# Loading weights later at two places, and additions into y on VectorE at the borders of the down groups

## The chip, the cores and the metric

One core of a Trainium2 chip runs the whole kernel as one program. The metric is the device time of an execution in microseconds (us); lower is better. Five engines work at the same time, each on its own list of instructions, in order: TensorE (PE) multiplies matrices, VectorE (DVE) and ScalarE (ACT) do arithmetic by element, GpSimd (POOL) does as well, and SyncE (SP) issues most of the transfers between device memory and on-chip memory. What one engine hands to another is awaited by semaphores.

## The reference

One step of a one-layer encoder on 1024 prompt frames and 64 sample frames (1088 columns in all, D = 1024), all in float32. Cut to what matters here:

```python
rq, rk, rv, rg, sq, sk, sv, ga, gb = split(rms_norm(x, g_attn) @ w_in)     # projections
A = retention(rope(rq), rope(rk), rv)                                      # 4 heads
B = sliding_window_attention(sq, sk, sv)                                   # 16 heads
x += (sigmoid(ga) * A_out + sigmoid(gb) * B_out) @ w_mix_out
x += cross_attn(x, memory K/V)
x += (silu(hn @ w_gate) * (hn @ w_up)) @ w_down                            # hn = rms_norm(x, g_ffn), D_FF = 2816
y = rms_norm(x, g_final)
```

The first product of the kernel is the retention V of one head, the second the retention K of the same head. The last large product is `@ w_down`, with the sum over the 2816 rows of `w_down` cut into three groups.

## The kernel before

Float32 values are multiplied in three passes: each operand is split into a high half, rounded to TensorE's float32r type by a cast on ACT, and a low half, the difference, by a subtraction on DVE (`split`, lines 122 to 124). A product then is hi x hi + hi x lo + lo x hi (lines 212, 213 and 215). All columns stand transposed, so weights are the stationary operand and the 1088 columns stream past in two halves (`HALF` = 544), each in two parts of 272.

Large products are done on 2x2 blocks: two output tiles by two halves of the columns (t), each a sum over two halves of the inner dimension (j). `plain` (line 232) does the eight block products as they stand, four inner tiles each, six matmuls per tile, so 24 matmuls per block product in the first two groups. `strassen` (line 254) does seven with sums of blocks as operands, and merges their results on DVE and ACT. The operands have names: B11, B12, B21, B22 are blocks, T1 to T4 are sums. The order of a Strassen product is P1 (B11), P2 (B21), P6 (T2), P5 (T1), P7 (T3), P3 (B22), P4 (T4). The weights come as a pair of raw tiles of 512 KB (tag `raw`, two buffers, loaded by SP). For Strassen, `weight_ops` (line 173) splits blocks of them and lets POOL form sums in place in the raw tiles (lines 190, 191, 193 and 196) between the splits: P1 and P2 need none, P7 needs line 190, P5 line 191, P6 line 193 and P3 line 196. Split weights sit in buffers `wq`.

Order: a scheduler lays each engine's list out ahead of time, by priority (order in the program) and by a simulated timeline in which an instruction that is not ready lets later ones pass. `tc.issue_after(ins)` adds that the instructions in its block that run on the engine of `ins` come behind `ins` in that engine's list. It adds no wait.

The start (`project_phase`, line 570, and `start_phase`, line 430): x comes in sixteen tiles (`xr`, four buffers), is scaled on ACT into `xg` and split into the operands. `first` holds the weights of V, split for `plain`; `values(first, 0, self.plain)` multiplies them and stores the four results through SP to `d_qkv` (lines 638 to 641). The next line loads and prepares the weights of K for the first Strassen product: `first = pair("w_k", 0)`.

The down product (`down`, line 1542): the activations of the feed-forward part were stored to `d_op` as ready blocks and sums for each of the three groups (`GROUPS` = 8, 8 and 6 tiles of 128 rows, gi = 0, 1, 2). For each group, m = 0, 2, 4, 6 walks over pairs of output tiles. m = 0 of groups 0 and 1 is `plain`, since it needs only the B operands, and the T operands are loaded behind it (`load_operand`, order T2, T1, T3, T4; each loads tiles `hl` and splits them); the rest is `strassen`. In m = 6 of groups 0 and 1, `refill` replaces each B operand by that of the next group as soon as its product is done (`turn`); B12 takes the place of T4, after the last product. This is the border of two groups. The results are added into `y`: of each emitted pair, one addition reads PSUM and is on DVE (line 1552); the other reads the merged partial result `sb` in SBUF and is on POOL for groups 0 and 1, on DVE for group 2 (line 1554).

Of the kernel before, what the change touches and what calls it, by code (L numbers as in the profile page):

```python
# [2 lines left out]

# [1 line left out]

# [16 lines left out]
KT = D // P  # L22
# [20 lines left out]
OPS = ("B11", "T1", "T2", "B21", "T3", "B22", "T4", "B12")  # L43
# [66 lines left out]
class Kernel:  # L110
# [459 lines left out]
    def project_phase(self):  # L570
        nc, tc, io = self.nc, self.tc, self.io
        with ExitStack() as ctx:
# [7 lines left out]
            first = self.start_phase(sctx)  # L580
# [3 lines left out]
            half = lambda t: slice(t * HALF, (t + 1) * HALF)  # L584
            flat = lambda o: o.rearrange("p b c -> p (b c)")

            def staged():
                count[0] += 1
                return stage[(count[0] - 1) % len(stage)]

            def taken(ps, sb):
                o = staged()
                if sb is None:
                    nc.scalar.copy(o, ps)
                else:
                    nc.vector.tensor_tensor(out=o, in0=ps, in1=sb, op=ALU.add)  # L596
                return flat(o)
# [39 lines left out]

            def values(w, h, by=self.strassen):
                def emit(i, t, ps, sb):
                    self.store(self.d_qkv[2, 2 * h + i, :, half(t)], taken(ps, sb))  # L640
                by(w, self.ops, emit)

            pair = lambda w, h: self.load_ops([io[w][2 * h + i] for i in range(2)])
            def queries(p):
# [8 lines left out]
                        self.store(d[:, 9:17, :], r(o[:, 32:]))  # L653
                return put

            values(first, 0, self.plain)
            first = pair("w_k", 0)
            sctx.close()
            stage, count = self.stage_tiles(), [0]
            with ExitStack() as rctx:  # L660
# [873 lines left out]
    def fetch(self, name, group):  # L1534
        n0 = sum(GROUPS[:group]) // 2
        for k in range(GROUPS[group] // 2):
            self.pools = self.pools[1:] + self.pools[:1]
            a = self.pools[0].tile([P, HALF], F32, tag="hl", name="hl")
            self.load(a, self.d_op[OPS.index(name), n0 + k])
            yield a  # L1540

    def down(self, starts):
        nc, io = self.nc, self.io
        self.rings[0].next = (self.rings[0].next - 2) % KT
        stage = self.ring_tiles(0, 2, "y", F32)
        y = [self.rstd_f] + [stage[i // 2][:, i % 2, :] for i in range(4)]
        y += [self.yp.tile([P, T], F32, name=f"y{i}") for i in range(3)]
        half = lambda m, t: y[m][:, t * HALF:(t + 1) * HALF]
        def add(m, i, t, ps, sb, by=nc.gpsimd):
            v = half(m + i, t).rearrange("p (b c) -> p b c", b=2)  # L1550
            if ps is not None:
                nc.vector.tensor_tensor(out=v, in0=ps, in1=v, op=ALU.add)
            if sb is not None:
                by.tensor_tensor(out=v, in0=sb, in1=v, op=ALU.add)

        begun = set()

        def complete(m, c0, n):
            acc, o = self.rstd[:, c0:c0 + n], y[m][:, c0:c0 + n]
            if c0 not in begun:  # L1560
                begun.add(c0)
                nc.scalar.activation(acc, o, AF.Square)
            else:
                sq = self.hl.tile([P, HALF], F32, tag="hl", name="sq")[:, :n]
                nc.scalar.activation(sq, o, AF.Square)
                nc.vector.tensor_tensor(out=acc, in0=acc, in1=sq, op=ALU.add)

        def load_half(tile, m, a, b):
            self.load(tile.rearrange("p (k m) -> p k m", m=P), io["w_down"][m, :, a:b, :])

        for gi, g in enumerate(GROUPS):
            last = gi == len(GROUPS) - 1
            f0, n = starts[gi], g * P // 2
            for m in range(0, KT, 2):
                def emit(i, t, ps, sb, m=m):
                    add(m, i, t, ps, sb, nc.vector if last else nc.gpsimd)
                    if last and t == 1:
                        complete(m + i, HALF, HALF)

                raws = [self.wp.tile([P, 1024], F32, tag="raw", bufs=2, name="raw") for i in range(2)]  # L1580
                for i in range(2):
                    load_half(raws[i][:, :2 * n], m + i, f0, f0 + g)
                if m == KT - 4 and not last:
                    for name in ("B11", "B21" if gi == 0 else "T2"):
                        self.ahead[name, gi + 1] = list(self.fetch(name, gi + 1))
                if gi == 0:
                    for i in range(2):
                        self.load(y[m + i], self.d_h[1][m + i])
                if m == 0 and not last:
                    self.plain(self.plain_weights(raws, n), self.ops, emit)  # L1590
                    for name in ("T2", "T1", "T3", "T4"):
                        self.load_operand(name, gi)
                else:
                    w = self.weight_ops(raws, n, ("P2", "P4") if last else ())
                    if m == KT - 2 and not last:
                        self.refill = lambda name, gi=gi: self.turn(name, 1) if gi == 0 else self.turn_last(name)
                    self.strassen(w, self.ops, emit, last)
                    self.refill = None
                    if m == 0:
                        for name in ("B21", "T4"):  # L1600
                            self.load_operand(name, gi)
                if last and m == KT - 4:
                    nc.scalar.activation(self.root[:, 0, :1], self.rstd[:, HALF:HALF + 1], AF.Sqrt)
        rest = []
        for m in range(0, KT, 2):
            raw = self.wp.tile([P, 1024], F32, tag="raw", bufs=2, name="raw")
            for i in range(2):
                load_half(raw[:, i * n:(i + 1) * n], m + i, f0 + g // 2, f0 + g)
            ring, slots = self.slots["B11" if m < 4 else "T1"]
            q = self.rings[ring].tile("wb", slot=slots[m // 2 % 2])  # L1610
            self.last_queued = self.split(raw[:, :2 * n], q[:, 0, :2 * n], q[:, 1, :2 * n])
            rest += [(m + i, q[:, :, i * n:(i + 1) * n], self.ops[("B21", "T4")[i]]) for i in range(2)]
        self.finish(y, rest)
# [182 lines left out]
```

## Time and profile before

| | before |
|---|---|
| median of 3 runs | 2211.39 us (2210.66 to 2214.1) |
| profiled execution | 2210.58 us |
| its span, first to last instruction | 2208.8 us |
| mean granted TensorE clock | 0.992 |
| PE busy | 2155.7 us (98%) |
| DVE busy | 1577.8 us (71%) |
| ACT busy | 875.8 us (40%) |
| POOL busy | 653.2 us (30%) |

In the lines of the timeline: start in us from the span's start, duration in us, engine and line of the kernel, operation, output<-input with shapes, count (neighbours of one kind are merged), and in brackets how long the engine had been idle before and what ended that. `SPq` is the issue of a transfer, not the transfer. In the view of groups, busy time and mean ns come first, then idle time and its releasers. In the view of waits: engine and line, whom it waited for, us in total, times, longest. L124 is the low half of any split, L123 the cast.

### The profile page before, as it was taken

To read this page: it belongs to the slowest core of one execution; us is meant where nothing else is said; L and a number is where in the kernel's file an instruction comes from. 1 tells how busy PE (TensorE), PEld (TensorE's weight loads), DVE (VectorE), ACT (ScalarE), POOL (GpSimd) and SP (SyncE) were. 2 spreads that over 40 slices of the span, in tenths; PEclk is the share of its full clock that TensorE was granted. 3 is DMA by queue.
4 is the path that set the end of the run, shared out by engine and by line. 5 is a ranking of instruction groups with operands and counts; after the bars stand their busy time and mean duration, and the time that the engine had idled before them with its cause. 6 is when DMAs were issued, how large, how long until landed. Compare 5 with 4: busy or idle time off the path is not lost.

```text
span 2208.8 us, 41446 instructions
## 1 busy us (share of the span) xinstructions
PE 2155.7 (98%) x16307; PEld 2089.8 (95%) x16307; DVE 1577.8 (71%) x2654; ACT 875.8 (40%) x1894; POOL 653.2 (30%) x442
## 2 busy tenths in 40 slices
PE   8999999999999998999999999999999999999996
PEld 8999999999999996779999999999999999999996
DVE  7996958776677668775455555768777776778498
ACT  7344424344344346553133333333322222344243
POOL 1322333332343122230000000014555555544440
PEclk9999999999999999999999999999999999999998
DMA  5534253445245476327443111422333332385233
GB/s 197 167 127 137 90 149 122 131 127 156 96 153 172 165 220 213 112 64 224 124 153 107 57 49 58 144 86 90 124 133 101 104 118 95 124 297 167 91 114 110
DMA packets 181444, 290.83 MB, mean 132 GB/s; under 512 B 40290, under 2 KB 109314, under 8 KB 181250
## 3 DMA queue, kind: packets, MB, share of 16 engines
q1 hardware_dynamic: 176706, 278.74, 39.5%
q10 hardware_dynamic: 4032, 7.80, 0.9%
q8 instruction: 129, 2.11, 0.4%
q0 software_dynamic: 512, 1.64, 0.2%
q14 instruction: 65, 0.53, 0.1%
HBM read 196.95 MB, written 91.16 MB: 130 GB/s over the span
## 4 chain that ended last, share of the span: by engine, by line
PE 80%; DVE 11%; DMA 4%; ACT 2%; issue 2%; POOL 1%; SPq 0%; DVEq 0%; ACTq 0%; POOLq 0%
PE pq L215 15%; PE pq L212 15%; PE pq L213 15%; PE pd L156 8%; PE pd L158 8%; PE pd L157 8%; DVE wq L124 1%; PE pout L1031 1%; PE pss L969 1%; DMA hl<-d_op 1%; DVE T L124 1%; DVE B L124 1%; PE pp L1008 1%; DMA qs<-d_qkv 1%; DVE stage L596 1%
## 5 line engine op out<-in xcount | busy, mean ns | idle before, releaser
L124 DVE TENSOR_TENSOR wq<-raw,wq 128x512 fp32r<-128x512 f32 (+1 forms) x499 | 441.2, 888 | 137.1 <-ACT wq L123 135.5
L123 ACT CAST wq<-raw 128x512 fp32r<-128x512 f32 (+1 forms) x499 | 303.6, 614 | 586.0 <-PE pq L215 244.8
L212 PE MATMUL pq<-T,wq 128*128 128x272 f32 x1832 | 490.8, 288 | 3.6 <-ACT wq L123 2.1
L213 PE MATMUL pq<-T,wq 128*128 128x272 f32 x1832 | 491.5, 288 | 0.0
L213 PE MATMUL pq<-B,wq 128*128 128x272 f32 x1592 | 429.6, 290 | 6.7 <-DVE B L124 6.7
L212 PE MATMUL pq<-B,wq 128*128 128x272 f32 x1592 | 427.4, 289 | 1.3 <-DVE stage L596 1.1
L215 PE MATMUL pq<-T,wq 128*128 128x272 f32 x1832 | 382.0, 289 | 0.9 <-DVE wq L124 0.9
L190 POOL TENSOR_TENSOR raw<-raw 128x512 f32<-128x512 f32 (+1 forms) x59 | 90.2, 1529 | 967.1 <-DVE rs_r L301 480.4
L212 PEld LDWEIGHTS pq<-T,wq 128*128 128x128 f32 x1832 | 344.1, 188 | 5.6 <-ACT wq L123 1.9
L213 PEld LDWEIGHTS pq<-T,wq 128*128 128x128 f32 x1832 | 344.1, 188 | 0.8 <-issue 0.7
L215 PE MATMUL pq<-B,wq 128*128 128x272 f32 x1592 | 332.8, 289 | 0.0
L213 PEld LDWEIGHTS pq<-B,wq 128*128 128x128 f32 x1592 | 300.7, 189 | 9.2 <-DVE B L124 8.3
L212 PEld LDWEIGHTS pq<-B,wq 128*128 128x128 f32 x1592 | 300.5, 189 | 1.8 <-ACT wq L123 1.3
L215 PEld LDWEIGHTS pq<-T,wq 128*128 128x128 f32 x1832 | 289.6, 189 | 1.6 <-DVE wq L124 1.1
L215 PEld LDWEIGHTS pq<-B,wq 128*128 128x128 f32 x1592 | 252.8, 190 | 0.8 <-issue 0.8
L259 DVE TENSOR_TENSOR u<-pq,u 128x544 f32<-128x544 f32 x177 | 127.5, 720 | 101.3 <-PE pq L215 100.4
L193 POOL TENSOR_TENSOR raw<-raw 128x512 f32<-128x512 f32 (+1 forms) x59 | 82.8, 1403 | 110.4 <-DVE wq L124 105.3
L596 DVE TENSOR_TENSOR stage<-pq,u 128x544 f32<-128x544 f32 x112 | 80.4, 718 | 34.6 <-PE pq L215 31.2
L191 POOL TENSOR_TENSOR raw<-raw 128x512 f32<-128x512 f32 (+1 forms) x59 | 90.4, 1533 | 3.5
L996 POOL TENSOR_TENSOR t<-t,den 128x768 f32<-128x768 f32 (+2 forms) x34 | 49.9, 1468 | 127.0 <-DVE den L994 51.9
L196 POOL TENSOR_TENSOR raw<-raw 128x512 f32<-128x512 f32 (+1 forms) x59 | 82.4, 1397 | 4.4
L990 ACT ACTIVATE t<-t,nm 128x192 f32<-128x192 f32 (+2 forms) x136 | 58.9, 434 | 45.5 <-DVE nm L985 45.5
(388 smaller groups left out, 4600.4 us busy)
## 6 DMA issues: line engine op xcount, KB each, us to landing
hl<-d_op SPq DMA_DIRECT2D x85, 272.0 KB, 4.7
d_qkv<-stage SPq DMA_DIRECT2D x44, 272.0 KB, 2.2
d_op<-stage SPq DMA_DIRECT2D x44, 272.0 KB, 2.1
d_op<-ht SPq DMA_DIRECT2D x44, 272.0 KB, 3.3
raw<-w_gate SPq DMA_DIRECT2D x22, 512.0 KB, 3.5
raw<-w_up SPq DMA_DIRECT2D x22, 512.0 KB, 3.7
raw<-w_down SPq DMA_DIRECT2D x16, 512.0 KB, 4.1
d_gate<-stage ACTq DMA_DIRECT2D x28, 272.0 KB, 2.9
```

Of the source, the lines that this page charges most:

```text
L123: self.last_cast = self.nc.scalar.copy(hi, src).ins
L124: return self.nc.vector.tensor_tensor(out=lo, in0=src, in1=hi.bitcast(F32), op=ALU.subtract).ins
L156: mm(ps, wh, xh, start=start, stop=False)
L157: mm(ps, wh, xl, start=False, stop=False)
L158: self.last_mm = mm(ps, wl, xh, start=False, stop=stop).ins
L190: tt(out=a11, in0=a11, in1=a21, op=sub)
L191: tt(out=a21, in0=a21, in1=a22, op=add)
L212: mm(ps[:, c, :HC], w[:, 0, ks], x[:, 0, cs], start=start, stop=False)
L213: mm(ps[:, c, :HC], w[:, 0, ks], x[:, 1, cs], start=False, stop=False)
L215: self.last_mm = mm(ps[:, c, :HC], w[:, 1, ks], x[:, 0, c * HC:(c + 1) * HC], start=False, stop=stop).ins
L259: add = lambda out, a, b: nc.vector.tensor_tensor(out=out, in0=a, in1=b, op=ALU.add)
L596: nc.vector.tensor_tensor(out=o, in0=ps, in1=sb, op=ALU.add)
```

## The change

There are three edits. At the start, the four stores of the first results are kept in a list and the weights of K are loaded under `issue_after` of the first of them, so that on SP they stand behind it. In `down`, the additions of line 1554 run on DVE also for m = 6 of groups 0 and 1. And for m = 2 of groups 0 and 1, the two weight loads are put behind the last load of operand T1 in SP's list; for that, `fetch` keeps the last load's instruction in `self.loaded`. No arithmetic, tile or transfer is added or removed.

```diff
             def values(w, h, by=self.strassen):
                 def emit(i, t, ps, sb):
-                    self.store(self.d_qkv[2, 2 * h + i, :, half(t)], taken(ps, sb))
+                    self.stores.append(self.load(self.d_qkv[2, 2 * h + i, :, half(t)], taken(ps, sb)))
                 by(w, self.ops, emit)
...
+            self.stores = []
             values(first, 0, self.plain)
-            first = pair("w_k", 0)
+            with tc.issue_after(self.stores[0]):
+                first = pair("w_k", 0)
...
             a = self.pools[0].tile([P, HALF], F32, tag="hl", name="hl")
-            self.load(a, self.d_op[OPS.index(name), n0 + k])
+            self.loaded = self.load(a, self.d_op[OPS.index(name), n0 + k])
             yield a
...
                 def emit(i, t, ps, sb, m=m):
-                    add(m, i, t, ps, sb, nc.vector if last else nc.gpsimd)
+                    add(m, i, t, ps, sb, nc.vector if last or m == KT - 2 else nc.gpsimd)
...
-                for i in range(2):
-                    load_half(raws[i][:, :2 * n], m + i, f0, f0 + g)
+                with self.tc.issue_after(self.loaded) if m == 2 and not last else nullcontext():
+                    for i in range(2):
+                        load_half(raws[i][:, :2 * n], m + i, f0, f0 + g)
...
                     for name in ("T2", "T1", "T3", "T4"):
                         self.load_operand(name, gi)
+                        if name == "T1":
+                            behind = self.loaded
+                    self.loaded = behind
```

(`load` and `store` issue the same instruction on SP; `load` returns it.)

More of the change, by code (lines that the diff above doesn't have):

```diff
@@ L1 @@
 import math
-from contextlib import ExitStack, contextmanager
+from contextlib import ExitStack, contextmanager, nullcontext
 import numpy as np
```

## Prediction

> **What bounds the kernel now.** I read the page first, then PE's waits and the windows view by stretch, then each engine's timeline at the three places that the change touches. The page:
>
> ```profile
> span 2208.8 us, 41446 instructions
> PE 2155.7 (98%) x16307; PEld 2089.8 (95%) x16307; DVE 1577.8 (71%) x2654; ACT 875.8 (40%) x1894; POOL 653.2 (30%) x442
> ```
>
> PE is busy nearly throughout, so an edit pays only where PE waits or runs at a low clock. PE's timeline shows such waits at the start and at the border from the first down group to the second; the list of PE's waits there and the windows view follow (in the latter the length, then busy time and count of PE, PEld, DVE, ACT, POOL, then the granted clock).
>
> ```profile
> 25.11 0.59 PE L213 MATMUL pq<-B,wq 128*128 128x272 f32 x1 [2.89 <-DVE B L124]
> 48.44 0.39 PE L212 MATMUL pq<-T,wq 128*128 128x272 f32 x1 [1.21 <-ACT wq L123]
> 2034.64 0.39 PE L213 MATMUL pq<-B,wq 128*128 128x272 f32 x1 [1.88 <-DVE B L124]
> ```
> ```profile
> PE pq L213 <- DVE B L124: 3.1, 3, 1.9
> ```
> ```profile
> 25.00:28.20 3.20, 3.08 (x12) 2.76 (x12) 3.20 (x7) 3.20 (x7) 0.00 (x0) 0.50 0.01 2
> 2009.00:2027.00 18.00, 18.00 (x146) 18.00 (x146) 15.04 (x22) 9.33 (x17) 3.42 (x2) 1.00 0.71 243
> 2032.70:2041.90 9.20, 6.11 (x26) 5.41 (x26) 9.20 (x11) 4.33 (x9) 4.79 (x3) 0.64 0.66 193
> ```
>
> An undisturbed stretch does 146 matmuls in 18 us, 0.123 us each; a product of 24 takes 2.95. At the border 26 took 9.2 us where 26 x 0.123 = 3.2 would do: 6.0 us lost, of which 3.1 are waits for the low halves of operand B12 and the rest is a low clock (0.64 in that row). DVE is busy all 9.2 us: it bounds this place. At the start 2.9 us of waiting for B21 (from 22.2 to 25.1) is followed by 12 matmuls in 3.2 us at clock 0.50, 1.7 us lost: 4.6 us.
>
> **Part 1: the second pair's weights at the start.** SP's queue, the landing time, DVE, then POOL, then the chain of waits:
>
> ```profile
> 12.69 0.33 SPq L117 DMA_DIRECT2D raw<-w_k  x1
> 32.60 11.55 SPq L120 DMA_DIRECT2D d_qkv<-early  x4
> ```
> ```profile
> raw<-w_k SPq DMA_DIRECT2D x4, 512.0 KB, 5.3
> ```
> ```profile
> 20.30 0.69 DVE L124 TENSOR_TENSOR wq<-raw,wq 128x512 fp32r<-128x512 f32 x1
> 21.54 1.81 DVE L124 TENSOR_TENSOR T<-xg,T 128x544 fp32r<-128x544 f32 x1
> 23.27 1.78 DVE L124 TENSOR_TENSOR B<-xg,B 128x544 fp32r<-128x544 f32 x1
> 28.12 0.71 DVE L124 TENSOR_TENSOR B<-xg,B 128x544 fp32r<-128x544 f32 x1
> 43.33 3.27 DVE L124 TENSOR_TENSOR T<-xg,T 128x544 fp32r<-128x544 f32 x5
> ```
> ```profile
> 21.22 1.55 POOL L190 TENSOR_TENSOR raw<-raw 128x512 f32<-128x512 f32 x1 [20.77 <-DMA xr<-xT]
> 43.50 4.24 POOL L193 TENSOR_TENSOR raw<-raw 128x512 f32<-128x512 f32 x1 [19.03 <-DVE wq L124]
> ```
> ```profile
> 1945.92 11.90 POOL L190 TENSOR_TENSOR raw<-raw 128x512 f32<-128x512 f32 x1 [19.91 <-DVE stage L1476]
> ```
> ```profile
> 47.77 1.14 ACT wq L123 x2
> ```
>
> Two loads of 512 KB go from 12.7 to behind the first store at 32.6; nothing is added. Out of DVE's stretch before B21 go the splits of P1 (the row at 20.30) and P2, 0.65 each at the pitch of the five-split row (3.27 / 5), and the collisions with POOL's L190 and the L191 behind it: 1.81 and 1.78 where a lone split takes 0.71, 1.1 each. P1's split and both collisions lie ahead of the end of B21's second split (25.05), which comes 2.8 us earlier, about when PE arrives: the wait and the cold clock behind it go. All 3.4 us lie ahead of the split at 28.12, which then ends at 25.4; PE, 12 matmuls (1.5 us) past 22.2, waits 1.7 for it. PE is 4.6 - 1.7, about 3 us, ahead, and the first store with it.
>
> What is late next: this pair's own weights. The store goes at about 29.5, the loads land 5.3 later, near 35, and P1 is split by 36.5. PE wanted P1 two products before 47.2 (where the wait of 1.21 began), at 41.3, and now wants it at 38.3. But L190 and L191 now run while DVE is in its long stretch of splits, which ended at 46.6 and now ends near 46.6 - 3.4 + 1.3 = 44.5. L190 got through in 1.55 at 21.22, with DVE paying; L193 took 4.24 and another L190 11.90, each until DVE paused. If POOL gets in early, the start gives the whole 3. If it must wait for the pause, L190 1.3, P7's cast and split 1.3, L193 1.3 and P6's cast 0.6 follow 44.5: 49.0, where the first of the two casts at 47.77 ended by 48.4: 0.6 lost. I take the middle, since the rows stand on both sides: **-1.5 us (-3.1 to +1)**.
>
> The Trainium skill, page "SBUF — State Buffer", section "SBUF: two separate sides", says that whichever of the two engines starts first holds the shared port pair for its whole instruction, and the other blocks. If that meant that POOL waits for one DVE instruction, the start would give the whole 3; the row of 11.90 does not agree.
>
> **Part 2: the border from group 0 to 1.** SP, DVE and POOL:
>
> ```profile
> 2027.05 12.60 SPq L117 DMA_DIRECT2D hl<-d_op  x10
> ```
> ```profile
> 2025.52 1.49 DVE L124 TENSOR_TENSOR T<-hl,T 128x544 fp32r<-128x544 f32 x1 [0.32 <-ACT T L123]
> ...
> 2029.48 2.52 DVE L124 TENSOR_TENSOR B<-hl,B 128x544 fp32r<-128x544 f32 x2
> ...
> 2033.15 3.23 DVE L124 TENSOR_TENSOR B<-hl,B 128x544 fp32r<-128x544 f32 x2
> 2036.31 1.79 DVE L124 TENSOR_TENSOR T<-hl,T 128x544 fp32r<-128x544 f32 x1
> 2038.03 1.34 DVE L124 TENSOR_TENSOR B<-hl,B 128x544 fp32r<-128x544 f32 x2
> ```
> ```profile
> 2132.08 0.71 DVE L1554 TENSOR_TENSOR y<-u,y 128x544 f32<-128x544 f32 x1
> ```
> ```profile
> 2024.73 1.70 POOL L1554 TENSOR_TENSOR y<-u,y 128x544 f32<-128x544 f32 x1 [10.32 <-issue]
> 2029.00 1.77 POOL L1554 TENSOR_TENSOR y<-u,y 128x544 f32<-128x544 f32 x1 [2.57 <-DVE y L1552]
> 2032.73 1.28 POOL L190 TENSOR_TENSOR raw<-raw 128x512 f32<-128x512 f32 x1 [1.96 <-DVE wq L124]
> 2033.96 1.84 POOL L1554 TENSOR_TENSOR y<-u,y 128x544 f32<-128x544 f32 x1
> ```
>
> Against 0.71 for one split and 1.34 for two, the DVE rows of 1.49, 2.52, 3.23 and 1.79 hold 0.8 + 1.2 + 1.9 + 1.1 = 5.0 us of collisions, each beside POOL's work: some 2.9 beside the three y additions, 2.1 beside L190 and L191 of the next weights. The change gives the additions to DVE, 0.65 of its pitch each (2132.08 is such a one in the last group), and by loading the next weights behind T1's loads it moves their L190, L191 and the split of their P1 out of this stretch.
>
> The splits of B12 are the pairs at 2033.15 and 2038.03. PE stopped for the first at 2034.64 - 1.88 = 2032.8, and after it would take one each 0.75 us (six matmuls): 2032.8, 2033.5, 2034.3, 2035.0. The first ended at 2034.6. Less 0.8, 1.2 and 0.9 of collisions and 0.65 of the weight split, plus two additions (1.3), it ends at 2032.4; the second 0.65 later, in time. Ahead of the third come a T split and, at worst, the last addition: 2035.0, some 0.9 late with what PE needs to start; the fourth is in time. The loss shrinks from 6.0 to about 0.9, which cools no clock if it took 1.9 to do so: **-5.1 us (-6.0 to -2)**. The bad end is where DVE's order puts more T splits ahead of B12. The moved weights go out behind T1's loads, which are among the ten from 2027.05 to 2039.7; with 5 us to land, they come by 2045 at the latest. They are wanted after the whole plain product, eight products of 2.95 from 2032.8 - 5.9: 2050.5. That product covers them.
>
> **Part 3: the border from group 1 to 2.** No load is moved here (the condition leaves out the last group); only the additions change engine. DVE, POOL and PE's waits:
>
> ```profile
> 2118.28 1.72 DVE L124 TENSOR_TENSOR wq<-raw,wq 128x384 fp32r<-128x384 f32 x1
> ...
> 2123.10 1.72 DVE L124 TENSOR_TENSOR wq<-raw,wq 128x384 fp32r<-128x384 f32 x1
> 2126.65 0.54 DVE L124 TENSOR_TENSOR wq<-raw,wq 128x384 fp32r<-128x384 f32 x1
> ```
> ```profile
> 2117.81 1.78 POOL L1554 TENSOR_TENSOR y<-u,y 128x544 f32<-128x544 f32 x1 [3.66 <-DVE y L1552]
> ```
> ```profile
> PE pq L212 <- DVE y L1552: 0.4, 1, 0.4
> ```
>
> Two collisions (1.72 for 0.54) cost 2.4; four additions cost 2.6. DVE breaks even, POOL is free earlier for the weight sums, and a PE wait of 0.4 can go: **-0.5 us (-1.5 to +2.6)**, the worse end if the additions all add to the path.
>
> **Part 4: the same moved load in group 0**, where PE has no wait now. ACT, the landing times of all w_down loads, PE:
>
> ```profile
> 1947.84 4.17 ACT L123 CAST T<-hl 128x544 fp32r<-128x544 f32 x6 [0.72 <-DMA hl<-d_op]
> ```
> ```profile
> DMA to landing us min/median/max: 2.3/3.5/8.7
> ```
> ```profile
> 1969.76 0.29 PE L212 MATMUL pq<-T,wq 128*128 128x272 f32 x1
> ```
>
> T1's casts are the first four at 1947.84, so T1's last load went out by about 1948; the weights follow, and land by 1957 even at 8.7. P1 is wanted two products before the first P6 matmul at 1969.76, at 1963.8; P1's and P7's casts and splits, L190 and L193 and P6's cast take some 6 us from 1957, to 1963: covered, **0**. The plain product is that cover; were the load out only after 1955, some 5 us would show.
>
> **Sum.** -1.5 - 5.1 - 0.5 = -7.1 on the profiled execution's 2210.58 (span 2208.8 and 1.8 around it): 2203.5. The median of the runs, 2211.39, lies 0.8 above it: 2204.3.
>
> **Rivals.** Each with the other parts as forecast.
>
> Start not gained: L190 and L191 starve, +0.6 instead of -1.5. The rows of 11.90 and 4.24 speak for it, that of 1.55 against. 2206.4, chance 0.14.
>
> Start gained in full: POOL gets the port after one instruction, -3.1. The row of 1.55 speaks for it alone. 2202.7, chance 0.10. This is the skill's rule as a case.
>
> The stores hold the weights: the loads end up behind all four, the last of which leaves by 44.1. They land at 49.4, P1 is cast at 50.0 where PE had it at 41.3; its split, L190, P7, L193 and P6 take 5.2 more, to 55.2, and PE's two products end at 55.9, against 48.4 now: +7.5 instead of -1.5. For it: SP is in order and the third store waits long (11.55 for four); against it: the order asked for is behind the first. 2213.3, chance 0.10.
>
> DVE is the bound at both borders and nothing is recouped, the splits colliding with POOL's remaining work as before. Eight additions of 0.65, 5.2 us, lie on the path, and 2.6 more of stall at half clock costs half of that again: +6.5 instead of -5.6, 2216.4, slower than before. It decides when the collisions saved fall under 0.65 per addition; about 1 each at the first border speaks against it, DVE busy in 9.2 of 9.2 us for it. Chance 0.12.
>
> Group 0 stalls as in part 4, +5: 2209.3. The slack speaks against it. Chance 0.06.
>
> **How the numbers follow.** The forecast keeps 0.48. About 0.2% (4.4 us) is what a measurement of this kernel can tell from no change. Faster than 2207.0 are the forecast, the full start and near half of the start not gained: 0.64. Slower than 2215.8 are the border rival and a little of the stores': 0.14. The rest, 0.22, is the same. The range goes from the good ends of the parts (-3.1 - 6.0 - 1.5 = -10.6, 2200.8, and 1.8 below it for group 0 and the last group, whose shorter collisions I did not count) to the stores' rival: 2199 to 2213. The forecast's own range is 2201 to 2207.
>
> **What would show it.** Right: in 2026 to 2042 no POOL y row, B12's splits near 0.71 each, PE's wait under 1 us and the clock at 1.00; at the start, w_k issued right behind the first store and no stretch of 0.50 near 25 to 28. Wrong: PE waiting for wq near 40 to 48 us for more than 1.2, PE waiting near 1964 to 1970, or a B12 wait still above 2 us.

## The result, and the profile after

| | before | changed |
|---|---|---|
| median, five runs each on one chip | 2212.46 us (2210.66 to 2214.1) | 2202.66 us (2202.32 to 2203.55) |
| profiled execution | 2210.58 us | 2202.32 us |
| its span | 2208.8 us | 2200.2 us |

The ratio is 0.9951, 95% interval 0.994 to 0.9963: 10 us or 0.5% faster, more than the 0.2% that can be told from no change. The forecast was 2204.3. The sum came out close, but two of its terms did not come as worked out, and one that is as large as the largest was missing. (The changed file is two lines longer from its second half on: the additions of L1554 are L1556, a product's first write into y is L1554 where it was L1552, kt's L764 is L766.)

The page of the changed kernel, to set beside the two lines shown of before:

```profile
span 2200.2 us, 41451 instructions
PE 2154.9 (98%) x16307; PEld 2089.9 (95%) x16307; DVE 1576.3 (72%) x2662; ACT 873.6 (40%) x1894; POOL 631.2 (29%) x434
```

Eight additions went from POOL (442 to 434) to DVE (2654 to 2662). PE's busy time is the same to 0.8 us; 8 us of its idle time are gone.

**The border from group 0 to 1.** PE's waits between 2015 and 2055 us, the window 9.2 us wide that corresponds to 2032.7:2041.9 of before, then DVE's and POOL's timeline:

```profile
PE pq L213 <- DVE B L124: 0.7, 3, 0.3
```
```profile
2028.60:2037.80 9.20, 8.51 (x64) 7.93 (x63) 9.09 (x15) 4.33 (x8) 0.80 (x1) 1.00 0.98 345
```
```profile
2024.34 1.35 DVE L124 TENSOR_TENSOR B<-hl,B 128x544 fp32r<-128x544 f32 x2
2025.62 0.72 DVE L1554 TENSOR_TENSOR y<-pq,y 128x544 f32<-128x544 f32 x1
2026.25 0.71 DVE L124 TENSOR_TENSOR T<-hl,T 128x544 fp32r<-128x544 f32 x1
2026.88 1.98 DVE L124 TENSOR_TENSOR B<-hl,B 128x544 fp32r<-128x544 f32 x3
2028.79 0.71 DVE L1556 TENSOR_TENSOR y<-u,y 128x544 f32<-128x544 f32 x1
2029.42 0.71 DVE L124 TENSOR_TENSOR B<-hl,B 128x544 fp32r<-128x544 f32 x1
...
2031.33 1.35 DVE L124 TENSOR_TENSOR B<-hl,B 128x544 fp32r<-128x544 f32 x2
```
```profile
2037.00 1.84 POOL L190 TENSOR_TENSOR raw<-raw 128x512 f32<-128x512 f32 x1 [30.36 <-DMA raw<-w_down]
```

Where 26 matmuls were done in 9.2 us at clock 0.64, 64 are done at 1.00. The B splits of this stretch take 0.66 to 0.71 each (1.98 for three, 0.71 for one, 1.35 for two); B12's are the last four of the eight, and in before a pair of them took 3.23. POOL does nothing for 30 us; the addition on DVE (2028.79) costs 0.71.

**The start.** SP's queue and PE's waits:

```profile
31.82 0.33 SPq L117 DMA_DIRECT2D d_qkv<-early  x1
32.20 0.42 SPq L117 DMA_DIRECT2D raw<-w_k  x1
32.67 0.45 SPq L117 DMA_DIRECT2D d_qkv<-early  x1
33.16 0.43 SPq L117 DMA_DIRECT2D raw<-w_k  x1
```
```profile
26.26 0.40 PE L213 MATMUL pq<-B,wq 128*128 128x272 f32 x1 [1.70 <-DVE B L124]
48.19 0.39 PE L212 MATMUL pq<-T,wq 128*128 128x272 f32 x1 [2.34 <-ACT wq L123]
78.66 0.39 PE L212 MATMUL pq<-T,wq 128*128 128x272 f32 x1 [1.61 <-DVE u L259]
```

In before the matmul of the first of these rows is the one at 28.89 (next row). Behind it stands the window of the changed kernel from 27 to 30 us:

```profile
28.89 0.40 PE L213 MATMUL pq<-B,wq 128*128 128x272 f32 x1 [0.69 <-DVE B L124]
```
```profile
27.00:30.00 3.00, 3.00 (x16) 3.00 (x15) 3.00 (x6) 3.00 (x6) 0.00 (x0) 0.52 0.00 0
```

The loads are out right behind the first store. The wait of 2.89 that ended at 25.11 is gone: PE does this matmul at 22.34. The 1.70 is the wait for the next split, 12 matmuls on, which in before is the 0.69 at 28.89. A stretch at about half clock is still there, now behind the 1.70. The wait for P6's weights rose from 1.21 to 2.34, and the one at 78.66 was 0.46 in before: nothing is left of the gain by 80 us.

**A place that the prediction did not name: 326 to 345 us.** PE waits here for kt, an operand of the last head. PE's timeline of before, then of the changed kernel, and two windows of 5 us of each in the same order:

```profile
336.43 0.55 PE L156 MATMUL pss<-qs,ks 128*128 128x256 f32 x1 [3.53 <-DVE kt L764]
```
```profile
331.35 0.36 PE L156 MATMUL pss<-qs,ks 128*128 128x256 f32 x1 [0.48 <-DVE kt L766]
```
```profile
331.00:336.00 5.00, 1.90 (x16) 1.68 (x14) 4.85 (x7) 1.19 (x4) 3.31 (x2) 0.95 0.56 143
336.00:341.00 5.00, 4.57 (x21) 4.60 (x22) 2.42 (x6) 1.69 (x4) 0.00 (x0) 0.50 0.47 141
```
```profile
331.00:336.00 5.00, 4.65 (x38) 4.68 (x39) 3.36 (x8) 2.21 (x5) 0.00 (x0) 1.00 0.63 181
336.00:341.00 5.00, 5.00 (x43) 5.00 (x42) 3.95 (x8) 4.28 (x11) 0.00 (x0) 1.00 0.32 86
```

Before loses 3.5 us of waiting and then runs at half clock (21 matmuls where 43 go). Upstream stand the weight loads w_k of this head. SP issued the store of the bias table (d_rb, 1 MB) just ahead of them in before; in the changed kernel, whose order of work was laid out anew from the start on, that store goes out 15 us ahead of them. SP's timeline of before and of the changed kernel, then, in the view of DMA issues, count, KB and median us to landing, in the same order:

```profile
307.24 0.66 SPq L120 DMA_DIRECT2D d_rb<-rb  x1
309.24 4.96 SPq L117 DMA_DIRECT2D raw<-w_k  x2
```
```profile
296.61 0.68 SPq L120 DMA_DIRECT2D d_rb<-rb  x1
312.07 1.62 SPq L117 DMA_DIRECT2D raw<-w_k  x2
```
```profile
d_rb<-rb SPq DMA_DIRECT2D x1, 1024.0 KB, 12.9
raw<-w_k SPq DMA_DIRECT2D x2, 512.0 KB, 11.3
```
```profile
d_rb<-rb SPq DMA_DIRECT2D x1, 1024.0 KB, 12.9
raw<-w_k SPq DMA_DIRECT2D x2, 512.0 KB, 5.0
```

The late weights put POOL's weight sums later (L190 at 323.43 against 318.54), and with them DVE's splits, behind which kt's product stands.

### The profile page after: what moved, and what is told of

Its sections match the earlier page's. It is cut to its first block, busy times and chain, and to the rows that moved or that the text cites. A ratio compares the mean times of both kernels' runs of the same rounds, so it can differ in the third digit from the quotient of the medians.

```text
span 2200.2 us, 41451 instructions
## 1 busy us (share of the span) xinstructions
PE 2154.9 (98%) x16307; PEld 2089.9 (95%) x16307; DVE 1576.3 (72%) x2662; ACT 873.6 (40%) x1894; POOL 631.2 (29%) x434
## 4 chain that ended last, share of the span: by engine, by line
PE 81%; DVE 10%; DMA 4%; ACT 2%; issue 2%; POOL 1%; SPq 0%; DVEq 0%; POOLq 0%; ACTq 0%
PE pq L215 16%; PE pq L212 16%; PE pq L213 16%; PE pd L156 8%; PE pd L158 8%; PE pd L157 8%; DVE wq L124 2%; PE pout L1033 1%; PE pss L971 1%; DMA raw<-w_k 1%; DMA hl<-d_op 1%; PE pp L1010 1%; DVE T L124 1%; PE pp L1020 1%; DVE B L124 1%
## 5 line engine op out<-in xcount | busy, mean ns | idle before, releaser
L190 POOL TENSOR_TENSOR raw<-raw 128x512 f32<-128x512 f32 (+1 forms) x59 | 84.2, 1428 | 1039.5 <-DVE rs_r L301 483.6
L193 POOL TENSOR_TENSOR raw<-raw 128x512 f32<-128x512 f32 (+1 forms) x59 | 80.5, 1364 | 89.9 <-DVE wq L124 80.1
L191 POOL TENSOR_TENSOR raw<-raw 128x512 f32<-128x512 f32 (+1 forms) x59 | 88.0, 1491 | 3.6
L196 POOL TENSOR_TENSOR raw<-raw 128x512 f32<-128x512 f32 (+1 forms) x59 | 83.7, 1419 | 4.4
```

Of the source, the lines that this page charges most:

```text
L190: tt(out=a11, in0=a11, in1=a21, op=sub)
L191: tt(out=a21, in0=a21, in1=a22, op=add)
L196: tt(out=a12, in0=a12, in1=a11, op=sub)
```

## The experiments

Theory: the border's gain is from the additions and the moved load, the start gives nothing by itself, and the 5 us at 326 to 345 are a knock-on of the start's edit through the place of d_rb's store. Rivals: the start's gain is a local one, carried along; the borders make up the whole.

All runs are listed in one table: the time of each stretch of the profiled execution less that of before. The stretches lie between named events of PE's timeline: the second block of `pk<-ident,ks` (123.4 us in before), the ninth (326.6), the tenth (345.1), the last (496.3), the last change from T to B operands ahead of group 0's plain product, m=2's first T product behind it (30 us later), the same two events at the border 0 to 1 (36.2 us), the change from T to B behind group 1's last product and the next change from T to B but one (21 us). "Rest" is the remainder of the down phase. The last column is the ratio of the run's times to those of before on the same chip, with its interval.

```
                     to 123 -326 -345 -496 -group0 group0  0-1  1-2  rest span   ratio (95%)
before, in us         123.4 203.2 18.4 151.2 1443.5  29.9 36.2 21.0 181.9 2208.8
changed                -0.4  -1.7 -5.7  +0.4   +3.0  +0.3 -4.8 -0.7  +0.9   -8.6  0.9951 (0.9940-0.9963)
changed, again         +1.6  -1.8 -4.4  +0.6   +4.3  +0.5 -5.6 -0.7  +1.9   -3.6  0.9945 (0.9928-0.9963)
start only             +1.4  -0.5 -5.7  +1.3   +3.9  +4.2 -0.6  0.0  +1.1   +5.0  0.9980 (0.9968-0.9992)
both down edits        +3.1  +1.0 -1.1  +0.9   +0.3   0.0 -6.1 -0.7  +2.2   -0.5  0.9975 (0.9963-0.9987)
additions only         +0.7  +0.2 -0.2  +0.5   -0.7  +2.5 -5.4 -0.7  -0.2   -3.4  0.9971 (0.9959-0.9982)
late load only         +2.0  -0.4 -0.8  +0.7   +1.2   0.0 -1.2 -0.1  +2.9   +4.4  0.9995 (0.9983-1.0007)
bias table later       +1.7  -2.8 -6.4  +2.0   -0.5  +2.4  0.0 -0.1  +0.8   -2.8  0.9972 (0.9961-0.9983)
first border's adds    +0.6  -0.5 -2.2  -0.2   +0.8   0.0 -6.3  0.0  +1.4   -6.6  0.9951 (0.9940-0.9963)
no late load           +0.1  -0.7 -4.8  +0.5   -0.6  +1.9 -6.2 -0.7  +2.7   -7.9  0.9947 (0.9935-0.9959)
bias later, down       +2.1  -1.4 -6.4  +2.1   +2.4  +0.7 -5.9 -0.7  +0.7   -6.4  0.9939 (0.9927-0.9951)
bias later, all        +2.3  -2.3 -6.4  +2.3   +1.7  +0.1 -5.9 -0.7  +2.3   -6.6  0.9946 (0.9933-0.9960)
small store            +5.1  -1.6 -6.4  +5.1   +1.8  +1.1 -0.8 +0.8  +2.6   +7.7  1.0003 (0.9991-1.0014)
behind x's loads       +3.8   0.0 -6.2  +2.3   +2.2   0.0 -5.6 -0.7  +0.4   -3.8  0.9954 (0.9938-0.9970)
```

Two things must be known to read it. The profiled execution of before was a quick one: its kernel's medians on the three later chips were 2214.58, 2215.9 and 2214.08, so its neighbours read some 4 us too high in "span". And the first column differs by 0.7 to 3.1 us from before in kernels whose order of work is before's up to 1930 us (both down edits, the additions, the late load), and by 5.1 in the small store's, which is before's up to 300 us: a single profile does not resolve 2 us there, while the columns of the borders repeat to 1 us.

**The start alone.** The two edits of the first part; the borders as before.

```diff
-            first = pair("w_k", 0)
+            with tc.issue_after(self.stores[0]):
+                first = pair("w_k", 0)
```

> The start edit alone (the first store kept, w_k loaded behind it), down as before. The traces of before and after put PE only 0.7 us ahead at 61 us, level again at 120 us, and 7.7 us ahead at 345 us, of which 5.3 are won between 326 and 345 us. Theory 'knock-on': the edit does not pay at its place but re-lays all later lists, and in the new order the bias table's store (12.9 us to land) no longer lies in front of the w_k load of the last head; PE's wait for kt near 333 us shrinks from 3.5 to about 0.5 us; time about 2208.5 us (-4), since some of it is given back by 1900 us. Rival 'local': the edit pays 1.5 us at the start and the gain at 345 us belongs to something else; time about 2211 us.

2210.74 us, 4 us below before. The first 326 us show no gain; 326 to 345 gives 5.7, as in the changed kernel. The knock-on stands, the local gain falls. What it gains there it loses in part in group 0 (below).

**Both edits at the down groups, without the start.**

```diff
-                    add(m, i, t, ps, sb, nc.vector if last else nc.gpsimd)
+                    add(m, i, t, ps, sb, nc.vector if last or m == KT - 2 else nc.gpsimd)
...
+                with self.tc.issue_after(self.loaded) if m == 2 and not last else nullcontext():
```

> Both down edits (additions on VectorE at the borders, weights of m = 2 behind T1's loads), start as before. Theory 'the borders pay': PE 4.8 us ahead after the border from group 0 to 1 and some 0.5 more after the next; time about 2207.5 us (-5). Rival 'one sum': the gain needs both halves of the change; then about 2211. Up to 1900 us its lists are those of before, so it also tells whether the 128x384 matmuls between 1010 and 1200 us go at 173.5 ns each (as in the trace of before) or 176.7 (as after): if the laid-out program decides that, 173.5.

2208.96 us, 5.6 below before: 6.1 at the first border, 0.7 at the second, 1.1 at 326 to 345, where its wait for kt stays.

**The additions alone** (the first of these two lines).

> Only the additions of m = 6 in groups 0 and 1 moved from GpSimd to VectorE. Theory 'collisions': 2.9 us of collisions go and 1.3 us of additions come ahead of the first B12 split, the lost 6.0 us at the border shrink to about 3.5, and the next border breaks even: about 2210 us (-2.5). Rival 'the load alone': VectorE is as late as before, 0 to -0.5: 2212. Rival 'VectorE is the bound': +2.6: 2215.

**The late load alone** (the second).

> Only the weights of m = 2 in groups 0 and 1 loaded behind T1's loads; additions stay on GpSimd. Theory 'collisions': L190 and L191 and one weight split leave the stretch (2.1 + 0.65 us), the first B12 split ends about 1.6 us earlier, the later ones more; the lost 6.0 us shrink to about 2.5: about 2209 us (-3.5). Rival 'additions alone': 0, 2212.5. In group 0 PE does not wait for the later weights (no PE wait between 1960 and 1972 us).

The times are 2207.75 us with the additions alone and 2214.43 us with the late load alone (0.9971 and 0.9995 of before): the first gave more than its theory's 2.5, the second did not give its 3.5. The additions alone give 5.4 at the first border, the late load alone 1.2 (the kernels with neither of the two show 0, -0.6, 0.0 and -0.8). POOL's timeline says why, first with the additions on DVE, then with the late load alone; behind them, in the same order, stand the windows that correspond to 2032.7:2041.9 of before:

```profile
2033.74 1.66 POOL L190 TENSOR_TENSOR raw<-raw 128x512 f32<-128x512 f32 x1 [22.39 <-DMA hl<-d_op]
2035.48 1.66 POOL L191 TENSOR_TENSOR raw<-raw 128x512 f32<-128x512 f32 x1
```
```profile
2028.01 1.69 POOL L1554 TENSOR_TENSOR y<-u,y 128x544 f32<-128x544 f32 x1 [10.47 <-PE pq L215]
2032.27 1.77 POOL L1554 TENSOR_TENSOR y<-u,y 128x544 f32<-128x544 f32 x1 [2.57 <-DVE y L1552]
```
```profile
2035.60:2044.80 9.20, 8.62 (x69) 8.40 (x68) 9.20 (x14) 3.78 (x7) 1.54 (x1) 1.00 0.78 249
```
```profile
2035.40:2044.60 9.20, 6.17 (x37) 5.91 (x37) 9.20 (x12) 4.79 (x9) 3.42 (x3) 0.84 0.98 355
```

In the first kernel L190 and L191 still stand in DVE's stretch and draw a pair of B12's splits out to 2.93 us (at 2034.79), but PE waits only 0.6 us, in one place, and keeps its full clock. In the second they are gone (L190 is at 2042.84), and still PE's two waits for B come to 3.0 and its clock falls to 0.84. It is the additions' collisions that matter here. With the additions on DVE the late load adds nothing at this border: -5.4 and -6.2 without it, -4.8 to -6.3 with it.

What the late load does is in the column "group 0". The six profiles with the early load (before, start, additions, bias table later, no late load, small store) show 0, 4.2, 2.5, 2.4, 1.9 and 1.1 us more than 29.9, the eight with the late load 0 to 0.7. In the start-only run, PE's and POOL's timeline:

```profile
1948.79 0.40 PE L213 MATMUL pq<-B,wq 128*128 128x272 f32 x1 [1.58 <-DVE B L124]
1951.15 0.60 PE L213 MATMUL pq<-B,wq 128*128 128x272 f32 x1 [0.71 <-DVE B L124]
```
```profile
1946.89 1.26 POOL L190 TENSOR_TENSOR raw<-raw 128x512 f32<-128x512 f32 x1 [20.25 <-DMA d_op<-stage]
1948.23 1.65 POOL L191 TENSOR_TENSOR raw<-raw 128x512 f32<-128x512 f32 x1
```

Here L190 gets in at once and DVE pays. It takes 1.26 to 1.62 us in all five profiles that show a stall; in before's the same L190 took 11.90 us, and PE waited for nothing. What decides between the two was not found: counted from the start of this stretch, L190 begins at 4.9 to 6.7 us in the five and at 6.1 in before.

**The bias table one head later.** The kernel before, none of the three edits; the store goes out behind a pair's weight loads.

```diff
-                    if h == 1:
+                    if h == 2:
                         self.later.append(self.bias_table)
...
+        with self.tc.issue_after(self.raw_load):
+            self.store(self.d_rb.rearrange("h (i c) -> h i c", c=512),
...
```

(`raw_load` is the last weight load that was issued.)

> The kernel before, without any of the three edits; only the bias table is taken up one head later, and the store of its broadcast copy (d_rb) is issued behind a pair's weight loads instead of just ahead of the fourth head's w_k. Theory (the stretch 326 to 345 us is won because that store no longer stands in front of the w_k loads; the start's edit only moved it there): the wait of PE for kt (3.5 us in before) and the half clock of 331 to 341 are gone, the stretch is 5 us shorter, and the time is 4 to 5 us below before, ratio about 0.998. Rival A (it is the start's new issue order as a whole, the store is a bystander): the stretch and the time stay, 0 +-1 us. Rival B (the store is long wherever it lies): the stretch is shorter, but a like wait shows at the load that now follows it, 0 to -2 us.

2208.23 us, 0.9972 of before, which by that ratio is 6 us (3.8 to 8.6 by its interval). Of the w_k loads at 309.29, in the view of DMA issues, and of the window where before had half clock:

```profile
raw<-w_k SPq DMA_DIRECT2D x2, 512.0 KB, 3.4
```
```profile
336.00:341.00 5.00, 5.00 (x43) 5.00 (x42) 3.47 (x7) 3.72 (x11) 0.00 (x0) 1.00 0.28 87
```

The stretch is 6.4 shorter without any edit at the start. 2.0 of it come back up to 496, where the table now stands: a part of the second rival.

**The small store.** The kernel before; the table stays, but its store in front of the w_k loads is cut to 4 of 32 copies, and the table is computed and stored whole a second time one head later.

```diff
+                    if h in (1, 2):
+                        self.later.append(lambda n=4 if h == 1 else 32: self.bias_table(n))
...
```

> The kernel before, with the bias table where it was but its store in front of the w_k loads cut to 4 of its 32 copies (128 KB for 1024 KB); the table is computed a second time one head later and stored whole behind a pair's weight loads. Everything else that the table brings stays in its old place. Theory (the bytes of that store hold up the w_k loads): w_k lands in 3.4 to 6 us in place of 11.3, the wait of PE for kt is below 1 us, the stretch 326 to 345 is 4 to 6 us shorter, and the time is 3 to 6 us below before (the second table costs up to 1 us). Rival (it is the other work of the table, its matmul, copies and loads, or the order around it): w_k lands in 11 us and the time stays, 0 to +1.

Locally as the theory has it: w_k lands in 3.6 us (row below), PE does not wait for kt, and the stretch is 6.4 shorter, with the table's other work where it was. So it is the size of that store (its bytes and its packets were cut together, and the two were not told apart). The time was missed: 2214.73, no different from before. In the profile 5.1 of the 6.4 are given back up to 496, 3 more than with one late table; how much of that is the second table's own work was not separated.

```profile
raw<-w_k SPq DMA_DIRECT2D x2, 512.0 KB, 3.6
```

**Bias table later with both down edits, without the start; and with all three.** The edits are those above, put together.

> The changed kernel without its edit at the start, and with the bias table later and its store behind the weight loads instead. Theory (the start's edit pays only through where that store falls): as fast as the changed kernel, 2201.5 to 2204, ratio to before 0.995 to 0.9965; the first 100 us are as in before. Rival (the edit at the start pays by itself and the store is a bystander): 5 us slower than the changed kernel, 2208, ratio 0.9975, like the two down edits alone.

> The changed kernel with all its edits, and the bias table later with its store behind the weight loads, as in the two runs before. Theory (the start's edit pays only by where that store falls): the two ways to move the store do not add, 2200.5 to 2203.5, within 1.5 us of the changed kernel and of the run without the start's edit. Rival (the start's edit has a gain of its own that the store's move leaves standing): 4 us or more below the run without the start's edit, near 2197.

2200.72 and 2203.35 us, 0.9939 and 0.9946 of before. The start's edit can be left out if the store is moved instead, and the two ways do not add: the start's edit pays by where it puts d_rb's store. That the first of them beats the changed kernel is not shown (their intervals overlap).

**The additions at the first border alone; and all without the late load.**

```diff
+                    add(m, i, t, ps, sb, nc.vector if last or m == KT - 2 and gi == 0 else nc.gpsimd)
```

> The changed kernel, but VectorE adds into y only at the border of groups 0 and 1; at the border of groups 1 and 2 GpSimd adds as before. Theory (the additions pay at the first border alone, and the 0.7 to 1.5 us won up to 2153 at the second are given back in the tail): the changed kernel's time, within 1 us, ratio to before 0.995 to 0.996. Rival A (at the second border they only delay the sums, the two waits of 1.0 us each at 2148 and 2151 are theirs): 1.5 to 2 us below the changed kernel. Rival B (they pay there too): 1 to 2 us above the changed kernel.

> The changed kernel without the later loading of the next sums' weights: start and additions alone. Theory (the late load takes away a stall in group 0 that an early load brings or not by the moment at which GpSimd's copies L190 start, 4.1 us in the start-only run and 2.4 us in the additions-only run; at the first border the additions alone give the whole gain): the stretch from group 0's plain half to m=2's T is 32 to 34 us against 30.0, the border 0 to 1 stays near 31, and the time is 2 to 4 us above the changed kernel, 2205 to 2207. Rival (the late load is needed at the border and not in group 0, as the prediction had it): group 0 stays 30.0, the border is 2 us longer, 2204.7. Rival (it does nothing): 2202.7, within 1 us.

2204.29 and 2203.04 us. At the second border all eight profiles with the additions there show -0.7, the five without 0.0, -0.1, -0.1, 0.0 and +0.8; "rest" is as large with them as without (means 1.4 and 1.8), so they do not hold the tail. Without the late load group 0 takes 1.9 more, as expected, but the time of the whole did not show it: 2203.04 stands below its neighbour's 2204.29, and 1.9 us is less than these runs tell apart.

**The w_k loads behind the last load of x**, near 22 us, with both down edits and the later table.

```diff
+            with tc.issue_after(self.last_x):
+                first = pair("w_k", 0)
```

> Both down edits and the later bias table, and the second pair's w_k loads issued right behind the last load of x, near 23 us: between before (12.7 and 14.5 us) and the changed kernel (32.2 and 33.2 us). Theory (before they make GpSimd collide with VectorE ahead of B21, in the changed kernel they come too late for P6's weights; between the two neither holds): PE's wait for B before B21 is 1.7 us or less for 2.9, its wait for P6's weights stays 1.2 us or less for 2.3, and PE is 1 to 2 us ahead of before at 60 to 90 us; the time is 1 to 2 us below the run without any edit at the start. Rival (GpSimd's copies then meet VectorE's next stretch, behind B21): the waits add to the same 3.5 to 4 us wherever the loads stand, and the time is that run's, within 1 us.

The first half came as the theory had it: the wait ahead of B21 is 1.70, P6's weights are on time, PE is 1.0 us ahead of before at 50 to 70. Then a wait for the next weights, 2.38 us at 72.68, takes it all; 2203.99 us. POOL's timeline:

```profile
33.19 8.66 POOL L190 TENSOR_TENSOR raw<-raw 128x512 f32<-128x512 f32 x1 [32.74 <-DVE wq L124]
```

L190 is on the engine for 8.66 us while DVE does twelve operations of 0.66 to 0.72 each from 33.02 to 40.70 without a pause, none of them slowed, and ends about 1 us after they do.

**The changed kernel once more.**

> The changed kernel itself, once more, to stand beside the others on one chip: 2202.7 within 2 us by every theory. Its stretch 326 to 345 tells whether the wait for kt comes back in other runs of it, as in the run with the first border's additions alone (2.5 us there, 0.5 us in the changed kernel's first profile), whose work up to then is the same.

2203.90 us. PE's wait for kt is 1.8 us here, 2.5 in the run with the first border's additions, 0.5 in the first profile (0.5 to 2.5 in the five profiles with the start's edit and the early table): the start's edit moves the store away far enough only in part, and the later table, with no wait in four of four profiles, does it in full.

## Why the prediction was right, and where it was not

**Part 2, the first border (-5.1; measured -4.8, and -5.8 on the mean of the nine profiles that have the additions):** right in size, place and signs. The splits near 0.7, no POOL addition, PE's wait of 0.7 and the clock of 1.00 are what it named. Its split of the 5.0 us of collisions into 2.9 for the additions and 2.1 for L190 and L191 was wrong as a split of the gain: the additions alone bring 5.4. With them gone L190 and L191 still collide with B12's splits, but PE waits only 0.6 for those and its clock stays at 1.00, so the low clock, some 2.9 of the 6.0 lost in before, goes with the additions alone. With only L190 and L191 gone, waits of 3.0 and a clock of 0.84 stay.

**Part 3, the second border (-0.5):** -0.7 in all eight profiles with the additions. The rival in which DVE becomes the bound at both borders fell.

**Part 4, group 0 (0):** "PE has no wait now" was read off the one profile of six in which the early load makes no stall. The others say 1.1 to 4.2, mean of the six 2.0, so in this stretch the moved load is worth about 2 us on average, not 0 (the times do not show it: 0.9975 with it and 0.9971 without it at the old start, 0.9951 and 0.9947 at the new); 0.3 more was measured in the changed kernel's profile against before's 29.9. The step that failed is a bound: L190's 11.90 us was quoted, and it was not asked what DVE and PE would do had it been 1.3.

**Part 1, the start (-1.5):** "PE is about 3 us ahead" held at the place for which it was worked out. Counting matmuls, the one that before does at 28.89 comes 2.6 us earlier in the changed kernel (2.4 to 3.5 in the six profiles with this edit), and the wait of 1.7 that the sum allowed for came as 1.70. The step that failed is "and the first store with it". DVE, with no collision and 0.72 for a split, is still busy without a pause from 18 to 34 us, and PE, now early, meets it again: in five of the six profiles it waits another 0.65 to 0.68 for a B split further on; in the first profile of the changed kernel its clock falls instead, to 0.52 from 27 to 30 us, where "no stretch of 0.50 near 25 to 28" had been set down as a sign of being right. The clock was 1.00 behind the same wait of 1.70 in the other five, so that wait alone does not decide it. The matmul that before does at 34 us comes only 1.4 us earlier (1.2 to 2.3). The first store leaves at 31.82 in place of the 29.5 worked out. What it named as next late then came: the wait for the weights near 48 was 2.34, over the 1.2 set down as the sign of failure. By 81 us PE is 1.2 to 3.0 us behind, at 123 within the spread. That is the rival "start not gained", through L190 as it had it: 3.59 us in the changed kernel (row below), and 8.66 where the loads came in between.

```profile
40.22 3.59 POOL L190 TENSOR_TENSOR raw<-raw 128x512 f32<-128x512 f32 x1 [39.77 <-DVE wq L124]
```

By the Trainium skill, page "SBUF — State Buffer", section "SBUF: two separate sides", whichever of the two engines starts first holds the shared port pair for its whole instruction, and the other blocks. Read as a wait of one instruction for POOL, it is not what the rows show: 8.66 us beside DVE operations of 0.7, as 11.90 before.

**What was missing:** -5.7 at 326 to 345. The prediction took the start's edit as local. It holds back two loads, and the order that is laid out behind them moves by a few places; one such move took a 12.9 us store away from in front of two loads. Nothing in before's lists of waits was hidden: 3.5 us for kt and two windows at clock 0.95 and 0.50 stood there, outside the places that were read. So -1.5 - 5.1 - 0.5 = -7.1 stands beside a profile of -8.6 that is made up of -0.4 to 123, -1.7 to 326, -5.7 to 345, +3.4 up to group 0, +0.3 in it, -4.8 and -0.7 at the borders and +0.9 in the rest. The right total owes 4 to 6 us to a term that it did not have: that much of it is luck.

## What to carry to other kernels

Here a store of 1 MB just ahead of weight loads on one queue made them land in 11 to 12 us in place of 3.4 to 6, and PE paid a product later, with a wait and half clock; ask of every large store what stands behind it. An edit at the start of a laid-out order is an edit of all that follows: read PE's waits over the whole span, and credit such a gain to the place where it falls before calling the edit good. A stretch that shows no wait in one profile may show 4 us in the next; where two engines collide, price both outcomes.

## What the runs showed of the hardware that was not expected

The matmuls of 128x384 between 1002 and 1211 us go at one of two paces, with nothing waiting. The groups by form from 1040 to 1200 us, of before and of the run with the late load alone, whose order of work up to there is the same (busy us, mean ns of one, idle time before):

```profile
L156 PE MATMUL pd<-mix,wq 128*128 128x384 f32 x128 | 43.0, 336 | 0.0
```
```profile
L156 PE MATMUL pd<-mix,wq 128*128 128x384 f32 x124 | 42.0, 339 | 0.0
```

The distance from one to the next is 173.5 ns in the first and 176.7 in the second, and the stretch is 2.4 us longer; the changed kernel has the slower pace in both its profiles (+2.3 and +2.4), the two down edits alone the quicker (+0.3), and so has the run with the first border's additions, whose order of work up to there is the changed kernel's. So no edit here decides it, and its cause stays open. In the changed kernel it makes up more than half of the +3.0 and +4.3 of the column "-group0".
